# Tile 41's first head, kept apart whole and made in ten pieces behind tiles 37 to 46

## The chip, the cores and the metric

The kernel runs on one core of a Trainium2 chip. A core has five engines with instruction streams of their own: TensorE (PE, matmuls, with PEld for its weight loads), VectorE (DVE), ScalarE (ACT), GpSimd (POOL) and SyncE (SP), which here only issues DMA transfers. PE writes to PSUM, a small memory that DMA can't read, so that results are copied from there to SBUF by ACT or DVE and sent to HBM from SBUF by 16 DMA engines. The engines wait for each other by semaphores alone. The metric is the device time of one execution in microseconds; for the kernel before it is 300.72 us (median of 3 runs, 300.61 to 300.89).

## The reference

```python
def setup_inputs():
    batch, n_heads, seq_t, seq_s, channels = 8, 12, 512, 512, 64
    ...

def reference(x: np.ndarray, y: np.ndarray) -> np.ndarray:
    return np.einsum('bhtc,bhsc->bhts', x, y).astype(np.float32)
```

For each of the 96 heads (batch by head), x is 512x64, y is 512x64, and the output is x times y transposed, 512x512 in float32. 25 MB come in and 100 MB go out.

## The kernel before

**Tiling.** The 96 heads are cut into NG = 6 groups of G = 16. A group of x or of y is one load of 2 MB into a slot, 128 partitions by 16 KB; eight partitions hold one head. `compress` casts a loaded slot to bf16 into `keep`; `mix` copies x from there into `xb`, and `transposes` turns `xb` and the kept y into `xT` and `yT` with 32x32 block transposes on DVE. There are two of each buffer, for the two halves of a group (unit i, NH = 12 units; unit i uses buffer i % 2).

**An output tile** holds two heads: a unit gives V = 4 tiles, so there are 48, numbered 0 to 47 (`o`). The 64 channels of a head use half of the 128 rows of PE, the two heads of a tile use both halves, and the matmuls of a tile put the two heads' rows on alternate partitions. Tile o is made for k = 0 to 7: k 0 to 3 into the PSUM buffer pm0 and k 4 to 7 into pm1, four banks each, which together is all of PSUM. `four` issues the four matmuls of one buffer. `result` has ACT copy pm0 and then pm1 into a slot of 2 MB, 128 partitions by 16 KB (L337), and `store` sends the slot to HBM from SP (L328). There are five slots for loads and results alike, so tile o waits for the store of tile o - 5.

**Order.** The instruction streams are written by hand: `emit` records for each step what it reads and writes, and puts in the waits that follow from that. ACT, DVE, POOL and SP get their instructions in program order. PE's are written last by `all_products`, a loop of six turns over eight tiles (j = o % 8), with register-valued waits on the semaphores `ev` (evictions by ACT) and `tr` (transposes). What doesn't fit the loop is recorded in `held` and issued inside an `If` on the turn.

**Tile 41** (SPLIT = 41) is stored in an own way. Its second head goes out of the slot as a whole (1 MB). Of its first head only k 0 and 1 go out of the slot (256 KB, pieces of 4 KB). The rest, k 2 to 7 (LEFT = 6), is made a second time by `corner`, right behind tile 41: three DVE copies pick single rows of x out of xT[0] into a piece of `keep` called `picked` (L275); 30 matmuls against the same y (L295) put these rows on chosen partitions, in eight groups of at most four that alternate between pm0 and pm1; DVE empties pm0 and ACT pm1 into `kept`, which lies over kept inputs that are no longer needed (L141 and L139); and three DMA issues (L314) send it: 4 partitions with 5 rows each from SP, 3 and 8 partitions with 4 rows each from POOL, in pieces of 12 KB (`FEW` has the partitions and the rows of each). The partitions are 0, 4, 8, 12; 20, 24, 28; and 64 to 92 in steps of 4; partition 16 is passed over. The eight groups are held behind tile 41's own products on PE, and a last wait in the held list keeps PE from tile 42's products until both buffers have been copied out. `prepare(i)` issues the transposes of unit i and the mixing copies of unit i + 1 on DVE; it stands behind the last tile of a unit, for the unit after the next.

Of the kernel before, what the change touches and what calls it, by code (L numbers as in the profile page):

```python
# [9 lines left out]
def kernel(  # L10
# [22 lines left out]
    nc = tc.nc  # L33
    B, H, T, C = x.shape
    _, _, S, _ = y.shape
# [3 lines left out]
    R = T // Q  # L39
    NG = B * H // G  # L40
# [5 lines left out]
    SLOTS = 5  # L46
    TURNS = NH // 2
    SPLIT = V * NH - 2 * V + 1
    LEFT = 6
    N = (K - LEFT) * S  # L50
    GROUP = 4
    FEW = ((0, 4, 5), (5, 8, 4), (16, 24, 4))
    fp32 = mybir.dt.float32
    bf16 = mybir.dt.bfloat16
    u32 = mybir.dt.uint32
# [52 lines left out]
    def emit(name, make, reads=(), writes=(), dma=None, lane=None, known_by=None, held=None):  # L108

        points = [writer[r] for r in (*reads, *writes) if r in writer]  # L110
        points += [v for w in writes for v in readers.get(w, ())]
        if name == "pool" and name in ticks:
            points.append((name, ticks[name]))
        need(name, points, known_by, held)
        p, step = (lane or name, 1) if dma is None else (f"dma{dma}", 16)
        if p not in sems:
            sems[p] = tc.alloc_semaphore(p)
        if held is not None:
            held.append(make)
        elif make is not None:  # L120
            make().then_inc(sems[p], step)
        at = (p, ticks.get(p, 0) + step)
        ticks[p] = at[1]
        snaps[at] = {**known[name], p: at[1]}
        if dma is None:
            for q in lanes.get(name, (name,)):
                snaps[at][q] = ticks.get(q, 0)
        for r in reads:
            readers.setdefault(r, []).append(at)
        for w in writes:  # L130
            writer[w], readers[w] = at, []

    made_slots, loaded, held = [], {}, []
    in_front = ["dve", "pool", "dve", "act"]

    def copy(name, dst, src, reads, writes):
# [9 lines left out]
    def both(i):  # L146
        return [("slot", i, 0), ("slot", i, 1)]
# [92 lines left out]
    def all_products():  # L240

        with nc.tensor.Fori(0, TURNS, 1) as t:
            for j in range(2 * V):
                if j % V == 0:
                    nc.tensor.wait_ge(sems["tr"], t * 2 + j // V + 1)
                for pm in range(2):
                    nc.tensor.wait_ge(sems["ev"], t * (4 * V) + 2 * j + pm + 1)
                    four(j, pm).then_inc(sems["pe"], 1)
                if j == SPLIT % (2 * V):
                    with nc.tensor.If(t == SPLIT // (2 * V)):  # L250
                        for step in held:
                            if callable(step):
                                step().then_inc(sems["pe"], 1)
                            else:
                                nc.tensor.wait_ge(sems[step[0]], step[1])

    def corner():

        half, h = divmod(SPLIT % (2 * V), V)
        xT = xTs[half].bitcast(bf16).rearrange("p (k h q u) -> p k h q u", k=K, h=V, u=2)  # L260
        yT = yTs[half].bitcast(bf16)
        most = max(many for _, _, many in FEW)
        kept = keep[:, :most * LEFT * S].bitcast(fp32)
        runs = kept.rearrange("p (j n) -> p j n", j=most)
        dst = ov[SPLIT // V, h][:, 0, N:]
        picked = keep[:, 3 * NG * R // 2 * D:].bitcast(bf16)[:, :most * LEFT * 96].rearrange(
            "p (j k m) -> p j k m", j=most, k=LEFT
        )
        under = [("yb", 1, b, ch) for b in range(NG - 3, NG - 1) for ch in range(2)]
        first = 0  # L270
        for lo, hi, many in FEW:
            rows = (hi - lo) * many
            emit(
                "dve",
                lambda: nc.vector.tensor_copy(  # L275
                    picked[:, :many, :, 4 * lo:4 * hi:4],
                    xT[:, K - LEFT:, h, first:first + rows, 0].rearrange("p k (e j) -> p j k e", j=many),
                ),
                [("xT", half)],
                [("picked", lo)] + (under if lo == 0 else []),  # L280
            )
            first += rows
        places = [[("xk", i)] for i in range(NG - 1)]
        for i in range(0, NG - 1, 2):
            places.append([("yb", 0, b, ch) for b in (i, i + 1) if b < NG - 1 for ch in range(2)])
        banks = [divmod(b, LEFT) for b in range(most * LEFT)]
        for g in range(0, len(banks), GROUP):
            part = banks[g:g + GROUP]
            pm = g // GROUP % 2
            m = 96 if part[0][0] < most - 1 else 16  # L290

            def make(part=part, pm=pm, m=m):

                for b, (j, k) in enumerate(part):
                    last = nc.tensor.matmul(  # L295
                        pms[pm][:m, b, :], picked[:, j, k, :m], yT[:, h * S:(h + 1) * S],
                        start=True, stop=True,
                    )
                return last

            emit("pe", make, [("picked", lo) for lo, _, _ in FEW] + [("yT", half)], [("pm", pm)], held=held)
            copy(
                "act" if pm else "dve", kept[:m, g * S:(g + len(part)) * S],
                pms[pm].rearrange("p j s -> p (j s)")[:m, :len(part) * S],
                [("pm", pm)], places[g // GROUP],
            )
        need("pe", [v for pm in range(2) for v in readers[("pm", pm)]], held=held)
        first = 0
        for lo, hi, many in FEW:
            rows = (hi - lo) * many  # L310
            name = "pool" if lo else "sp"
            emit(
                name,
                lambda: engines[name].dma_start(  # L314
                    dst[first:first + rows].rearrange("(e j) n -> e j n", j=many),
                    runs[4 * lo:4 * hi - 3:4, :many],
                ),
                reads=[w for place in places for w in place],
                dma="side" if lo else "corner",
            )  # L320
            first += rows

    def store(o, s):
        i, h = divmod(o, V)
        to, src = ov[i, h], slots[s]
        parts = [(to, src)] if o != SPLIT else [(to[:, 1], src[1::2]), (to[:, 0, :N], src[0::2, :N])]
        for to, src in parts:
            emit("sp", lambda: nc.sync.dma_start(to, src), reads=both(s), dma=s)  # L328

    def result(o, s):  # L330

# [22 lines left out]
    with tc.tile_critical():  # L354
        sems["ev"] = tc.alloc_semaphore("ev")
        ticks["ev"] = 2
        nc.scalar.sem_inc(sems["ev"], 2)
        for g in range(SLOTS):
            load(g)
        emit(  # L360
            "pool",
            lambda: nc.gpsimd.dma_start(  # L362
                spare[0:17:4, :, :D // 2], xv[0, 0:5].rearrange("p (a b c) -> p a b c", a=2, c=D)[:, :, 0, :D // 2]
            ),
            writes=["spare"],
            dma="side",
        )
        for half, name in enumerate(("dve", "pool")):
            emit(
                name,  # L370
                lambda: engines[name].memset(xbs[half], 0.0),  # L371
                writes=[("xb", half, part) for part in range(4)],
            )
        front = []
        for n in range(2 * NG):
            if n == 11:
                result(3, slot())
            compress(n)
            mix(n // 4, "pool", n % 4)
            if n == 4:  # L380
                transposes(0)
            if n < 5:
                load(n + SLOTS)
            elif n in (6, 8):
                load(n // 2 + 7)
            elif n < 10:
                front.append(slot())
            if n > 7 and n < 11:
                result(n - 8, front[n - 8])
            if n == 9:  # L390
                transposes(1)
        prepare(2)
        for o in range(V, V * NH):
            result(o, slot())
            if o == SPLIT:
                corner()
            if o % V == V - 1:
                prepare(o // V + 2)
        all_products()
        need("pool", [("dmaside", ticks["dmaside"])])  # L400
        need("dve", [("dmacorner", ticks["dmacorner"])])
        for i, name in enumerate(("dve", "dve", "dve", "dve", "act")):
            need(name, [(f"dma{i}", ticks[f"dma{i}"])])
# [30 lines left out]
```

## Time and profile before

| | us |
|---|---|
| median of 3 runs | 300.72 (300.61 to 300.89) |
| the profiled execution | 300.63 |
| its span | 298.8 |
| ACT busy | 217.9 (73%) |
| DVE busy | 161.6 (54%) |
| PE busy | 144.7 (48%) |
| POOL busy | 57.9 (19%) |
| DMA, mean rate over the span | 421 GB/s |
| granted TensorE clock, mean | 0.773 |

The span goes from the first to the last instruction of the program; the device time has some more around it. Lines of the profile name an engine, an operation, output<-input by the program's names, and shapes. "L141" is the line of a helper (`copy`), which all copies share, so these are told apart by their tiles and shapes: `keep<-pm` is a copy of the corner, `xb<-keep` one of `mix`, `keep<-slot` one of `compress`. "L139" is the same helper's branch for ACT. In the timeline, a line gives start, length, engine, line, operation and count, and in brackets how long the engine had been idle and what ended that.

### The profile page before, as it was taken

Reading aid. Unit: us, or ns where it says so; the run is one execution under the profiler, and the core shown is the slowest. Engines: PE = TensorE matmul, PEld = TensorE weight load, DVE = VectorE, ACT = ScalarE, POOL = GpSimd, SP = SyncE. Lnnn points to the kernel's source line nnn. Section 1 sums busy time; section 2 is a strip of 40 time slices with the busy share of each in tenths; the row PEclk is TensorE's granted clock in tenths of the full one; section 3 lists DMA queues with packets and bytes.
Section 4 is the critical chain, followed back from the end, with each engine's and each line's share of the span. In section 5 each row is a group of like instructions: output and inputs, shape, how many; then the busy total and the mean of one; then the engine's idle time right before and its main releaser. Section 6 shows DMA issues by size and latency. Waiting matters only on the chain.

```text
span 298.8 us, 1363 instructions
## 1 busy us (share of the span) xinstructions
PE 144.7 (48%) x408; PEld 39.3 (13%) x414; DVE 161.6 (54%) x80; ACT 217.9 (73%) x113; POOL 57.9 (19%) x26
## 2 busy tenths in 40 slices
PE   0000040547665663867475665676475667475400
PEld 0000010111111110211111111111111112121100
DVE  2167897999929594915809439076292535600000
ACT  1665676999999996786868686767777775589900
POOL 3399999991000000000000000000000000010000
PEclk9999995657789997565956767756857767979965
DMA  7999999999999999999999999999999999999997
GB/s 265 430 428 432 430 430 428 428 432 432 425 432 430 434 428 429 434 430 428 430 432 429 432 436 428 430 436 423 425 432 434 430 421 428 421 388 430 421 421 316
DMA packets 8875, 125.87 MB, mean 421 GB/s; under 512 B 1128, under 2 KB 1128, under 8 KB 1192
## 3 DMA queue, kind: packets, MB, share of 16 engines
q1 hardware_dynamic: 8680, 125.29, 98.6%
q0 software_dynamic: 192, 0.54, 0.5%
q8 instruction: 1, 0.02, 0.0%
q14 instruction: 2, 0.02, 0.0%
HBM read 25.17 MB, written 100.66 MB: 421 GB/s over the span
## 4 chain that ended last, share of the span: by engine, by line
DMA 54%; ACT 27%; issue 5%; PE 4%; DVE 3%; another core or an unknown queue 1%; SPq 0%; ACTq 0%
DMA out_dram<-slot 41%; ACT slot L337 25%; DMA slot<-in_y_dram 7%; DMA slot<-in_x_dram 6%; DVE keep L141 3%; ACT keep L139 2%; PE pm L295 2%; PE pm L234 2%; SPq L157 0%; ACTq L101 0%; SPq L429 0%; SPq L354 0%
## 5 line engine op out<-in xcount | busy, mean ns | idle before, releaser
L337 ACT ACTIVATE slot<-pm 128x2048 f32<-128x2048 f32 x96 | 173.7, 1894 | 38.2 <-DMA out_dram<-slot 35.0
L234 PE MATMUL pm<-yT,xT 128*128 128x512 bf16 x378 | 135.6, 502 | 132.0 <-ACT slot L337 92.4
L206 DVE STREAM_TRANSPOSE xT<-xb 128x2048 uint32<-128x2048 uint32 x12 | 46.8, 3897 | 69.4 <-PE pm L234 67.0
L234 PEld LDWEIGHTS pm<-yT,xT 128*128 128x128 bf16 x384 | 35.9, 114 | 230.7 <-ACT slot L337 152.0
L139 ACT ACTIVATE keep<-slot 128x4096 bf16<-128x4096 f32 (+1 forms) x12 | 36.5, 3044 | 21.5 <-DMA slot<-in_x_dram 16.3
L141 DVE COPY xb<-keep 32x2048 bf16<-32x2048 bf16 x36 | 47.0, 1305 | 1.0
L141 DVE CAST keep<-slot 64x2048 bf16<-64x2048 f32 x12 | 36.1, 3010 | 17.1 <-DMA slot<-in_y_dram 16.9
L314 POOL DMA_DIRECT2D out_dram<-keep x2 | 1.1, 558 | 192.6 <-DVE keep L141 192.6
L141 POOL COPY xb<-keep 32x2048 bf16<-32x2048 bf16 x12 | 36.2, 3017 | 9.2 <-ACT keep L139 8.4
L215 DVE STREAM_TRANSPOSE yT<-keep 128x1024 uint32<-128x1024 uint32 x12 | 23.1, 1928 | 0.0
L141 POOL CAST keep<-slot 64x2048 bf16<-64x2048 f32 x6 | 17.8, 2973 | 1.4 <-DMA slot<-in_y_dram 0.8
L141 DVE COPY keep<-pm 96x2048 f32<-96x2048 f32 (+1 forms) x4 | 9.1, 2285 | 10.5 <-PE pm L295 10.5
L295 PE MATMUL pm<-yT,keep 128*96 128x512 bf16 (+1 forms) x30 | 9.2, 446 | 4.9 <-DVE keep L141 2.8
L139 ACT ACTIVATE keep<-pm 96x2048 f32<-96x2048 f32 (+1 forms) x4 | 6.6, 1657 | 5.4 <-PE pm L295 5.4
L295 PEld LDWEIGHTS pm<-yT,keep 128*96 128x96 bf16 (+1 forms) x30 | 3.4, 130 | 11.0 <-DVE keep L141 4.5
L371 DVE MEMSET xb<- 128x2048 uint32 x1 | 1.8, 1765 | 1.4 <-SPq L354 1.4
L139 ACT ACT_TABLE_LOAD x1 | 1.3, 1283 | 1.0 <-SPq L354 1.0
L371 POOL MEMSET xb<- 128x2048 uint32 x1 | 1.8, 1823 | 0.0
L362 POOL DMA_DIRECT2D spare<-in_x_dram x1 | 0.7, 701 | 1.2 <-SPq L354 1.2
L275 DVE COPY keep<-xT 128x120 bf16<-128x120 bf16 (+2 forms) x3 | 0.7, 355 | 0.0
L418 POOL MEMSET const-float32-0.0<- 128x1 f32 x1 | 0.1, 98 | 0.2 <-issue 0.2
L418 POOL MEMSET const-float32-1.0<- 128x1 f32 x1 | 0.1, 98 | 0.0
(2 smaller groups left out, 0.2 us busy)
## 6 DMA issues: line engine op xcount, KB each, us to landing
out_dram<-slot SPq DMA_DIRECT2D x47, 2048.0 KB, 20.5
slot<-in_x_dram SPq DMA_DIRECT2D x6, 2048.0 KB, 17.7
slot<-in_y_dram SPq DMA_DIRECT2D x6, 2048.0 KB, 20.8
out_dram<-slot SPq DMA_DIRECT2D x1, 1024.0 KB, 16.9
out_dram<-keep POOLq DMA_DIRECT2D x1, 384.0 KB, 6.1
out_dram<-slot SPq DMA_DIRECT2D x1, 256.0 KB, 18.6
out_dram<-keep SPq DMA_DIRECT2D x1, 240.0 KB
out_dram<-keep POOLq DMA_DIRECT2D x1, 144.0 KB, 5.6
```

The costliest lines, as they stand in the source:

```text
L139: lambda: nc.scalar.activation(dst, src, COPY)
L141: else engines[name].tensor_copy(dst, src),
L206: lambda: nc.vector.transpose(xTs[half].rearrange("p (k r e) -> p k e r", k=K, e=E), xbs[half].rearrange("p (k e c) -> p k e c", k=K, e=E),),
L215: lambda: nc.vector.transpose(yTs[half].rearrange("p (r j) -> p j r", r=D), ybs[half][b].rearrange("p (j c) -> p j c", c=D),),
L234: last = nc.tensor.matmul(pms[pm][:, b, :], xT[:, 4 * pm + b, h, :], yT[:, h * S:(h + 1) * S], start=True, stop=True,)
L275: lambda: nc.vector.tensor_copy(picked[:, :many, :, 4 * lo:4 * hi:4], xT[:, K - LEFT:, h, first:first + rows, 0].rearrange("p k (e j) -> p ...
L295: last = nc.tensor.matmul(pms[pm][:m, b, :], picked[:, j, k, :m], yT[:, h * S:(h + 1) * S], start=True, stop=True,)
L314: lambda: engines[name].dma_start(dst[first:first + rows].rearrange("(e j) n -> e j n", j=many), runs[4 * lo:4 * hi - 3:4, :many],),
L337: lambda: nc.scalar.activation(slots[s][:, k * S:(k + 4) * S], pms[pm].rearrange("p j s -> p (j s)"), COPY),
L362: lambda: nc.gpsimd.dma_start(spare[0:17:4, :, :D // 2], xv[0, 0:5].rearrange("p (a b c) -> p a b c", a=2, c=D)[:, :, 0, :D // 2]),
L371: lambda: engines[name].memset(xbs[half], 0.0),
L418: nc = _bacc.Bacc("TRN2", target_bir_lowering=False, num_devices=1)
```

## The change

`LEFT` is gone: all eight k of tile 41's first head are kept apart (1 MB, pieces of 16 KB), and `store` sends only the second head of tile 41 out of the slot. `corner` is split in three. `pick` copies the rows of x for all eight k, behind tile 35 and its `prepare`; `picked` now lies in `xb[0]`, whose last use is over by then. `piece(o)` stands behind each of the tiles 37 to 46 (BEGIN = 37, GROUPS = 10): four matmuls into pm0, one copy of pm0 by DVE into `kept`, and a wait of PE for that copy. The last two pieces have 16 rows, the others 96. `send` issues the three kept stores behind tile 46. `held` has one list for each of the ten tiles, each in an `If` of its own in PE's loop.

```diff
-    LEFT = 6
-    N = (K - LEFT) * S
     GROUP = 4
+    BEGIN = SPLIT - 4
     FEW = ((0, 4, 5), (5, 8, 4), (16, 24, 4))
+    GROUPS = -(-max(many for _, _, many in FEW) * K // GROUP)
...
-                if j == SPLIT % (2 * V):
-                    with nc.tensor.If(t == SPLIT // (2 * V)):
-                        for step in held:
-                            if callable(step):
-                                step().then_inc(sems["pe"], 1)
-                            else:
-                                nc.tensor.wait_ge(sems[step[0]], step[1])
+                for o in held:
+                    if o % (2 * V) == j:
+                        with nc.tensor.If(t == o // (2 * V)):
+                            for step in held[o]:
+                                if callable(step):
+                                    step().then_inc(sems["pe"], 1)
+                                else:
+                                    nc.tensor.wait_ge(sems[step[0]], step[1])
...
+    kept = keep[:, :most * K * S].bitcast(fp32)
+    picked = xbs[0].bitcast(bf16)[:, :most * K * 96].rearrange(
+        "p (j k m) -> p j k m", j=most, k=K
+    )
...
+    def piece(o):
...
+        g = o - BEGIN
+        part = [divmod(b, K) for b in range(most * K)][g * GROUP:(g + 1) * GROUP]
+        m = 96 if part[0][0] < most - 1 else 16
...
+            for b, (j, k) in enumerate(part):
+                last = nc.tensor.matmul(
+                    pms[0][:m, b, :], picked[:, j, k, :m], yT[:, h * S:(h + 1) * S],
+                    start=True, stop=True,
+                )
...
+        emit(
+            "pe", make, [("picked", lo) for lo, _, _ in FEW] + [("yT", half)], [("pm", 0)], held=held[o]
+        )
+        copy(
+            "dve", kept[:m, g * GROUP * S:(g * GROUP + len(part)) * S],
+            pms[0].rearrange("p j s -> p (j s)")[:m, :len(part) * S],
+            [("pm", 0)], places[g],
+        )
+        need("pe", readers[("pm", 0)], held=held[o])
...
-        parts = [(to, src)] if o != SPLIT else [(to[:, 1], src[1::2]), (to[:, 0, :N], src[0::2, :N])]
-        for to, src in parts:
-            emit("sp", lambda: nc.sync.dma_start(to, src), reads=both(s), dma=s)
+        if o == SPLIT:
+            to, src = to[:, 1], src[1::2]
+        emit("sp", lambda: nc.sync.dma_start(to, src), reads=both(s), dma=s)
...
             result(o, slot())
-            if o == SPLIT:
-                corner()
+            if BEGIN <= o < BEGIN + GROUPS:
+                piece(o)
+            if o == BEGIN + GROUPS - 1:
+                send()
             if o % V == V - 1:
                 prepare(o // V + 2)
+            if o == BEGIN - 2:
+                pick()
```

## The prediction

> **What bounds the kernel now.** I read the page's forty slices first, then the windows, then the timeline of ScalarE (ACT) and of the last third, and last the chain that ended last. The slices say that the DMA engines are the bound:
>
> ```profile
> PEclk9999995657789997565956767756857767979965
> DMA  7999999999999999999999999999999999999997
> GB/s 265 430 428 432 430 430 428 428 432 432 425 432 430 434 428 429 434 430 428 430 432 429 432 436 428 430 436 423 425 432 434 430 421 428 421 388 430 421 421 316
> ```
>
> All 16 DMA engines are busy from the second slice to the last, at about 430 GB/s. Only one slice, at 261 to 269 us, falls to 388. The windows put the hole there (columns: window, its length, busy us and count of PE, PEld, DVE, ACT, POOL, then granted clock, DMA share, GB/s):
>
> ```profile
> 125.00:224.00 99.00, 62.10 (x162) 15.80 (x164) 55.12 (x32) 73.82 (x41) 0.00 (x0) 0.69 1.01 430
> 265.00:270.00 5.00, 3.19 (x13) 0.93 (x12) 0.00 (x0) 5.00 (x4) 0.00 (x0) 0.95 0.84 347
> ```
>
> A full DMA share reads 1.01, so 5.00 x (1.01 - 0.84) / 1.01 = 0.8 us of DMA time were lost there, and nowhere else after the start. The timeline of ACT, which makes every output tile, shows why:
>
> ```profile
> 224.80 3.65 ACT L337 ACTIVATE slot<-pm 128x2048 f32<-128x2048 f32 x2 [1.31 <-DMA out_dram<-slot]
> 229.70 3.65 ACT L337 ACTIVATE slot<-pm 128x2048 f32<-128x2048 f32 x2 [1.25 <-DMA out_dram<-slot]
> ...
> 244.49 3.65 ACT L337 ACTIVATE slot<-pm 128x2048 f32<-128x2048 f32 x2 [1.30 <-DMA out_dram<-slot]
> 249.99 1.87 ACT L139 ACTIVATE keep<-pm 96x2048 f32<-96x2048 f32 x1 [1.85 <-PE pm L295]
> ...
> 262.71 21.35 ACT L337 ACTIVATE slot<-pm 128x2048 f32<-128x2048 f32 x12 [2.51 <-remote]
> ```
>
> Tiles 37, 38 and 41 start at 224.80, 229.70 and 244.49. A tile takes ACT 3.65 us, then ACT sits idle until a slot is free: each tile waits for the store of five tiles earlier, and these land 4.9 us apart. Behind tile 41 come the eight groups of the corner, and tile 42 starts only at 262.71, 18.2 us after tile 41 where 4.9 was the pace. That nearly costs nothing because the stores run far ahead:
>
> ```profile
> 223.52 20.89 DMA out_dram<-slot
> 244.41 0.02 issue
> ```
>
> This is the chain of waits: tile 36's store was issued at 223.52 and landed at 244.41, four stores deep in the queue. Its sixteen landings in the trace run from 242.23 to 244.41. A store onto an empty queue takes less: tile 42's, issued at 266.38, has its first packets 1.87 us later and lands at 273.17, 6.8 in all. So after tile 37's store (issued 228.47) the fastest DMA engine had 242.23 - 1.87 - 228.47 = 11.9 us in hand before tile 38's store was needed. This **lead** is what the corner spends, and what the change spends.
>
> **The change, part by part.** The question is how long a tile takes when a piece stands behind it, and whether ten such tiles spend more than the lead. The parts have these rows:
>
> ```profile
> 218.65 1.89 PE L234 MATMUL pm<-yT,xT 128*128 128x512 bf16 x4 [0.64 <-ACT slot L337]
> 246.51 1.03 PE L295 MATMUL pm<-yT,keep 128*96 128x512 bf16 x4 [1.38 <-ACT slot L337]
> 247.59 2.29 DVE L141 COPY keep<-pm 96x2048 f32<-96x2048 f32 x1 [6.16 <-PE pm L295]
> ...
> 258.76 2.28 DVE L141 COPY keep<-pm 16x2048 f32<-16x2048 f32 x1 [1.12 <-PE pm L295]
> 261.40 0.84 PE L234 MATMUL pm<-yT,xT 128*128 128x512 bf16 x3 [2.25 <-DVE keep L141]
> ```
>
> Four matmuls take 1.03 us at the full clock and 1.89 at half, 1.08 and 1.93 to the start of what waits for them. A copy out of PSUM on DVE takes 2.29 us whether 96 or 16 partitions are used.
>
> Every piece goes through pm0, the PSUM half that also takes k 0 to 3 of every tile, and the held list ends with a wait of PE for that copy. So from one tile's first eviction to the next tile's first eviction stand in one chain, each waiting for the one before: ACT empties pm0 (1.88); PE enters the branch (0.14, from ACT's end at 246.37 to 246.51); four matmuls of the piece; DVE copies (2.29); PE leaves the branch and starts the next tile (0.36, from 261.04 to 261.40); four matmuls of the tile; ACT may start. Behind PE's wait are all of the next tile's products, those into pm1 too. ACT's second eviction lies beside the piece and costs nothing. Fixed part: 1.88 + 0.14 + 2.29 + 0.36 = 4.67. The two groups of four depend on the clock: 6.83 us a tile at the full clock, 8.53 at half. In 125 to 224 us, with eight matmuls in 4.9 us, the granted clock was 0.69; the chain has twelve in about 7.8, nearly the same density with gaps of the same kind. I take that row: 0.69 is half clock for 62% of the time, 0.62 x 1.93 + 0.38 x 1.08 = 1.61 a group, and the **cycle** is 4.67 + 3.21 = 7.88 us, against the 4.9 at which the DMA engines take a tile away.
>
> Other edits. The three picks move from behind tile 40's preparation to tile 35's and take 8 planes in place of 6: 0.73 x 8 / 6 = 0.97 us on DVE, behind the mixing copies that end at 225.84. They end at 226.8 where the first piece could start at 224.80 + 1.88 + 0.14 = 226.82: nothing, at worst 0.3. The transposes for tiles 44 to 47 (3.88 + 1.90 us) stand on DVE between the copies of pieces 39 and 40; the second copy would be ready 0.36 + 1.61 + 1.88 + 0.14 + 1.61 = 5.6 us after the first, so it waits 0.2 (1.3 at full clock, 0 at half). The four copies taken from ACT (6.6 us) were inside the corner and go with it. Tile 41's 256 KB part goes from SP's queue and its bytes come with the kept rows: the bytes in all are the same. The three kept stores move from behind tile 41 to behind tile 46. On SP the kept store waits for piece 46's copy, 1.88 + 0.14 + 1.61 + 2.29 = 5.9 us after tile 46's first eviction starts; only tile 47's store is behind it, which isn't ready before 7.88 + 3.67. On POOL only its final wait is behind the two others.
>
> What they do to the end: tile 46's store is issued 3.67 us after its first eviction starts (228.47 against 224.80) and, onto an empty queue, lands 6.8 later. SP's kept store is 4 partitions of five 16 KB pieces. A tile is 8 packets of 16 KB on each of 16 engines in 4.9 us, 0.61 each; how the 4 partitions are spread no row shows. Spread over all engines the 320 KB take 0.8 us, on one engine each 3.06. The 5 landings of the 240 KB store of before (four of them data) are nearest to one engine each, so I take 3.06. Then tile 47's store takes 4.9. From tile 46's start to the last landing: 3.67 + 6.8 + 3.06 + 4.9 = 18.4.
>
> The **sum**: tile 37 starts at 224.80 as before, since up to there only untaken branches are new, on a PE that waits for ACT. Nine cycles, 70.9, and 0.2 for the transposes: tile 46 starts at 295.9. The last landing is at 314.3 where it was 297.68, so 16.6 later. Span 298.8 + 16.6 = 315.4; the profiled execution took 300.63 for a span of 298.8, so 1.83 more: **317.3 us**. That execution stands 0.09 under the median of the runs, 300.72. Cross-check by the lead: nine tiles lose 7.88 - 4.9 each, 26.8; the lead pays 11.9, less 2.45 for tile 41's store, which is half as long; a hole of 17.4 us opens. All at full clock: 61.5 + 1.3, end 306.0, 309.0 us. All at half: 76.8, and tile 47's own cycle decides (8.53 + 3.67 + 6.8 = 19.0): end 320.6, 323.5 us.
>
> **The rivals.** *Full clock.* The same chain at 6.83 us, 309.0 us. For it: in the corner and after it the clock was 0.84 to 1.00, with gaps of 1.3 to 2.3 us between groups. Against it: there PE was denser (33 matmuls in the 16 us from 246, against 12 in 7.9 here), and at the pace of 125 to 224, where the gaps in the timeline are 0.6 to 2.1 us, it was 0.69. The Trainium skill (TensorE: Matmul & The Clock Gate, "HAM oscillation — how this bites in real kernels") has it that PE stays warm while no idle gap exceeds about 3.4 us; by that rule, with the longest gap here at 2.7 us, the full clock would hold and the time would be 309. The trace of before speaks against the rule as a sufficient one.
>
> *Half clock throughout*: 323.5. For it, the wider gaps; against it, the clock records go up to full every 10 to 14 us even at the pace of before.
>
> *The pieces hide* (not slower). ACT is idle 1.3 us a tile, DVE for 9 us at a time, and 11.9 us of lead stand ready. If the cycle stayed under (297.7 - 18.4 - 224.80) / 9 = 6.06 us, the DMA engines would never run dry, the hole of 0.8 us would close and the time be 299.8 to 300.6. It needs 0.8 us less than the full-clock cycle, so a step must leave the chain: PE not waiting for the copy, say. Against it: the wait is in the held list, and no row of the chain can overlap another on the same half of PSUM.
>
> **How the numbers follow.** Mixed clock 0.75, full clock 0.13, half clock 0.08, hidden 0.04, shared between faster and no change. A measurement of this kernel tells about 0.2% (0.6 us) from no change. Every clock gives slower, so slower is 0.96. The range goes from just under the full-clock end to just under the half-clock end, 308 to 322.
>
> **What would show it.** Right: ACT's first evictions of tiles 38 to 47 about 7.9 us apart with PE as what ended their idle time, not the DMA; a granted clock near 0.7 there; DMA share under 0.8 from about 265 us on; tile 47's store issued near 307; the kept stores behind tile 46's. Wrong: evictions still 4.9 us apart (the pieces hide), or a cycle under 7 with the clock at 0.9 (full clock), or a last landing more than 4 us after tile 47's store should have landed (the kept stores cost more than one engine's five packets).

## The result, and the profile after

The changed kernel takes 324.89 us (median of 6 runs, 324.12 to 326.14) against 300.67 for the kernel before (6 runs, 300.55 to 300.97): a ratio of 1.0805, 95% interval 1.0784 to 1.0826. It is slower, as forecast, but by 24 us and not by 17, and beyond the upper end of the range. The profiled execution took 324.97 us, its span is 323.1.

The forty slices of the changed kernel:

```profile
PEclk9999999996999996568567765765677777777655
DMA  7999999999999999999999999999999965666771
GB/s 284 432 426 430 434 428 424 430 430 434 426 430 434 426 435 426 434 430 432 431 426 436 424 436 430 428 434 428 424 424 430 428 290 241 278 260 260 322 265 63
```

Up to slice 32, 258 us, the DMA engines are as full as before. Then they run at 241 to 322 GB/s for seven slices, and in the last one nearly dry. The timeline of ACT from tile 36 on gives the reason for the first part (start, length, and in brackets how long ACT had been idle and what ended it):

```profile
219.86 3.65 ACT L347 ACTIVATE slot<-pm 128x2048 f32<-128x2048 f32 x2 [1.25 <-DMA out_dram<-slot]
224.80 3.65 ACT L347 ACTIVATE slot<-pm 128x2048 f32<-128x2048 f32 x2 [1.29 <-DMA out_dram<-slot]
233.68 3.65 ACT L347 ACTIVATE slot<-pm 128x2048 f32<-128x2048 f32 x2 [5.23 <-PE pm L234]
241.65 3.65 ACT L347 ACTIVATE slot<-pm 128x2048 f32<-128x2048 f32 x2 [4.32 <-PE pm L234]
...
296.50 3.65 ACT L347 ACTIVATE slot<-pm 128x2048 f32<-128x2048 f32 x2 [3.92 <-PE pm L234]
304.06 3.65 ACT L347 ACTIVATE slot<-pm 128x2048 f32<-128x2048 f32 x2 [3.92 <-PE pm L234]
```

From tile 38 on ACT no longer waits for a store but for PE. Tile 46 starts at 296.50: nine cycles of 7.97 us in the mean, against 4.9 before. The chain that ended last shows one such cycle link by link (start, length, what; L347 is ACT's emptying, L234 a tile's matmuls, L297 a piece's):

```profile
288.94 1.89 ACT slot L347
290.87 1.04 PE pm L297 x4
291.93 2.29 DVE keep L141
294.22 0.35 issue
294.57 1.90 PE pm L234 x4
296.50 1.89 ACT slot L347
```

ACT empties pm0, PE makes the piece, DVE copies it out, PE leaves the branch, PE makes the next tile's half, ACT may start: no link of this chain lies beside another. The end of the kernel is in the windows (after the length come busy us of the five engines, then granted clock, DMA share, GB/s):

```profile
306.00:310.00 4.00, 0.00 (x0) 0.00 (x0) 0.00 (x0) 1.71 (x1) 0.00 (x0) 0.50 0.67 266
310.00:314.00 4.00, 0.00 (x0) 0.00 (x0) 0.00 (x0) 0.00 (x0) 0.00 (x0) 0.50 1.08 381
314.00:318.00 4.00, 0.00 (x0) 0.00 (x0) 0.00 (x0) 0.00 (x0) 0.00 (x0) 0.50 0.21 78
318.00:321.50 3.50, 0.00 (x0) 0.00 (x0) 0.00 (x0) 0.00 (x0) 0.00 (x0) 0.50 0.16 70
```

From 318 us a DMA share of 0.16 is left: some three of the 16 engines still work. Tile 47's store was issued at 307.73, and its sixteen landings in the trace are eight at 314.2 to 314.4, four at 315.5 to 316.7, one at 318.1 and three at 321.9. One of the last three engines carried this, from the trace's packets, joined where one starts as another ends:

```
queue   bytes        start    end
POOL's  65536        306.37   309.27
SP's    40960        309.27   310.79
SP's    40960        310.79   312.31
POOL's  65536        312.30   316.68
SP's    16384 x 8    316.69   321.55
```

Two of the eleven runs of 64 KB that POOL's two kept stores consist of, this engine's share of SP's kept store between them, and then the eight packets of tile 47. In the kernel before the kept pieces were 12 KB each; here the rows of a partition touch each other in `kept` and in the output, and the build made one run of 64 KB (POOL) or two of 40 KB (SP) out of them.

### The profile page after: what moved, and what is told of

The parts are those of the page before. It is cut to its first block, busy times and chain, and to the rows that moved or that the text cites. A ratio compares the mean times of both kernels' runs of the same rounds, so it can differ in the third digit from the quotient of the medians.

```text
span 323.1 us, 1437 instructions
## 1 busy us (share of the span) xinstructions
PE 156.3 (48%) x412; PEld 43.7 (14%) x424; DVE 175.5 (54%) x86; ACT 211.9 (66%) x109; POOL 57.9 (18%) x26
## 4 chain that ended last, share of the span: by engine, by line
DMA 43%; ACT 22%; DVE 12%; PE 12%; issue 5%; SPq 0%; ACTq 0%; DVEq 0%
DMA out_dram<-slot 30%; ACT slot L347 20%; DVE keep L141 9%; PE pm L234 8%; DMA slot<-in_y_dram 6%; DMA slot<-in_x_dram 6%; PE pm L297 4%; ACT keep L139 2%; DVE xb L141 2%; DVE xT L206 1%; DVE yT L215 1%; SPq L157 0%; DVE xb L277 0%; ACTq L101 0%; SPq L443 0%
## 5 line engine op out<-in xcount | busy, mean ns | idle before, releaser
L347 ACT ACTIVATE slot<-pm 128x2048 f32<-128x2048 f32 x96 | 174.3, 1885 | 73.6 <-PE pm L234 43.4
L234 PE MATMUL pm<-yT,xT 128*128 128x512 bf16 x372 | 143.8, 537 | 143.4 <-ACT slot L347 77.8
L234 PEld LDWEIGHTS pm<-yT,xT 128*128 128x128 bf16 x384 | 39.1, 121 | 244.8 <-ACT slot L347 126.9
L141 DVE COPY keep<-pm 96x2048 f32<-96x2048 f32 (+1 forms) x10 | 22.9, 2285 | 45.7 <-PE pm L297 45.7
L297 PE MATMUL pm<-yT,xb 128*96 128x512 bf16 (+1 forms) x40 | 12.5, 442 | 5.6 <-ACT slot L347 3.3
L297 PEld LDWEIGHTS pm<-yT,xb 128*96 128x96 bf16 (+1 forms) x40 | 4.6, 138 | 16.4 <-ACT slot L347 10.5
L277 DVE COPY xb<-xT 128x160 bf16<-128x160 bf16 (+2 forms) x3 | 1.0, 425 | 0.0
```

Of the source, the lines that this page charges most:

```text
L141: else engines[name].tensor_copy(dst, src),
L234: last = nc.tensor.matmul(pms[pm][:, b, :], xT[:, 4 * pm + b, h, :], yT[:, h * S:(h + 1) * S], start=True, stop=True,)
L277: lambda: nc.vector.tensor_copy(picked[:, :many, :, 4 * lo:4 * hi:4], xT[:, :, h, first:first + rows, 0].rearrange("p k (e j) -> p j k e", ...
L297: last = nc.tensor.matmul(pms[0][:m, b, :], picked[:, j, k, :m], yT[:, h * S:(h + 1) * S], start=True, stop=True,)
L347: lambda: nc.scalar.activation(slots[s][:, k * S:(k + 4) * S], pms[pm].rearrange("p j s -> p (j s)"), COPY),
```

## The experiments

The first eight tell apart what the cycle and what the end cost; the last looks for a version that is faster than both. The kernel before took 300.42 to 300.55 us in the median on the same chips, 300.07 to 302.00 in single runs. Where no number of runs is given, a version ran once, so a few tenths say nothing there.

**1. A gap between the kept rows.** 32 words after each row, so that rows no longer merge.

```diff
-    kept = keep[:, :most * K * S].bitcast(fp32)
+    PITCH = K * S + 32
+    kept = keep[:, :most * PITCH].bitcast(fp32)
...
-            "dve", kept[:m, g * GROUP * S:(g * GROUP + len(part)) * S],
+            "dve", kept[:m, g // 2 * PITCH + g % 2 * GROUP * S:g // 2 * PITCH + (g % 2 + 1) * GROUP * S],
...
-        runs = kept.rearrange("p (j n) -> p j n", j=most)
+        runs = kept.rearrange("p (j n) -> p j n", j=most)[:, :, :K * S]
```

> The changed kernel with 32 words left free between the kept rows, so that the kept stores go out as pieces of 16 KB and not as runs of 64 and 40 KB that were merged over rows. Theory: tiles 37 to 46 are made at the pace of before (71.7 us from tile 37's first eviction to tile 46's), and the 7.3 us by which the last store landed later than foreseen are two runs of 64 KB (2.90 and 4.38 us) on each of three DMA engines that also carry 80 KB of SP's kept store. In pieces they spread, and the time falls from 325.0 to 317.7 (317.0 to 318.5), with the last store's sixteen landings within 1 us. Rival: the tail is long because the kept stores stand last, ahead of tile 47's store, whatever their form: 324 to 326.

Measured: 317.78 us, the last store's landings from 314.2 to 314.8, tile 46 again at 296.49. So 7.2 us of the loss belong to the form of the kept stores, and 17.2 are left for the cycle. The windows of this run have no thin tail:

```profile
310.00:314.00 4.00, 0.00 (x0) 0.00 (x0) 0.00 (x0) 0.00 (x0) 0.00 (x0) 0.50 0.97 410
314.00:315.90 1.90, 0.00 (x0) 0.00 (x0) 0.00 (x0) 0.00 (x0) 0.00 (x0) 0.50 0.00 0
```

**2. No pieces.** On top of the first: `pick` and `piece` return at once.

> As the first, but the picks, the ten groups of matmuls and their copies are left out; the kept stores send what lies in their place. Theory: nothing is left in the chain between two tiles, the tiles come at 4.9 us, the DMA engines never run dry, and the time is 299.8 to 300.8. Rival: the kept stores behind tile 46 or the branches cost something by themselves: 303 or more.

Measured: 300.41 us. The tiles come 4.9 us apart again, with the stores as what ends ACT's waits:

```profile
259.89 3.65 ACT L353 ACTIVATE slot<-pm 128x2048 f32<-128x2048 f32 x2 [1.27 <-DMA out_dram<-slot]
264.79 3.65 ACT L353 ACTIVATE slot<-pm 128x2048 f32<-128x2048 f32 x2 [1.25 <-DMA out_dram<-slot]
```

So the loss of the cycle comes with the pieces. Of the kept stores this run says less. Only SP's stands behind tile 46 here: POOL has no copies left to wait for, and its two were issued at 75 us. The fourth run is nearer: POOL's are issued at 277 us, some 5 us ahead of tile 46's store, and SP's behind it, all in pieces of 16 KB. POOL's issues in this run and in the fourth:

```profile
75.14 1.11 POOL L330 DMA_DIRECT2D out_dram<-keep  x2 [6.43 <-ACT keep L139]
```

```profile
277.20 1.11 POOL L328 DMA_DIRECT2D out_dram<-keep  x2 [208.57 <-DVE keep L141]
```

The fourth run takes 300.14 us, so kept stores in pieces of 16 KB, issued that late, cost nothing that can be told. The second run is also a bound: without any hole in the DMA engines' work, and with ten groups less, its time can't be told from before.

**3. Half of each copy**, on the changed kernel itself.

```diff
-            "dve", kept[:m, g * GROUP * S:(g * GROUP + len(part)) * S],
-            pms[0].rearrange("p j s -> p (j s)")[:m, :len(part) * S],
+            "dve", kept[:m, g * GROUP * S:g * GROUP * S + len(part) * S // 2],
+            pms[0].rearrange("p j s -> p (j s)")[:m, :len(part) * S // 2],
```

> The changed kernel, but each copy of a piece on DVE takes only the first half of its columns (the other half is not copied). Theory: the copy is a link of the chain from tile to tile, so 2.29 us become about 1.2, nine times: 9.8 us less, 315.2 (314 to 316.5), and the cycle falls from 7.9 to 6.8 us. Rival: the pace is set by PE (its clock and its branches) and the copy lies beside it: 323 or more.

Measured: 312.66 us, 12.3 less and not 9.8. The copy took 1.22 us, 1.07 less, as the theory has it; but the mean cycle fell by 1.36, from 7.97 to 6.61. The other 0.29 is PE's: with less time between its groups the granted clock rose, and the tile's four matmuls took 1.53 us in the mean where they took 1.83, while the piece's stayed at 1.32. The windows of the changed kernel (from 224) and of this run (from 225):

```profile
224.00:245.00 21.00, 11.47 (x31) 3.64 (x30) 8.46 (x8) 10.64 (x6) 0.00 (x0) 0.72 1.01 429
245.00:270.00 25.00, 14.17 (x36) 4.55 (x36) 13.68 (x6) 11.23 (x7) 0.00 (x0) 0.73 0.76 323
```

```profile
225.00:265.00 40.00, 22.62 (x69) 7.53 (x68) 15.60 (x13) 21.87 (x12) 0.00 (x0) 0.80 1.01 427
```

So the copy is a link of the chain, and the shorter link paid a second time here, by the clock. The rival falls.

**4. Five pieces**, behind every second tile.

```diff
-            if BEGIN <= o < BEGIN + GROUPS:
+            if BEGIN <= o < BEGIN + GROUPS and (o - BEGIN) % 2 == 0:
```

> As the first, but with only the pieces behind tiles 37, 39, 41, 43 and 45 (the other five are left out). Theory: a tile with a piece takes 7.9 us, one without 3.5 to 4.0 as it is behind; tile 46 starts at 279 to 281 us, just where the lead of the stores is used up, and the time is 300.4 to 302.0: half the pieces cost almost nothing. Rival: every piece costs its delay, in proportion: half of the loss, 309.

Measured: 300.14 us, a little under the expected range; proportion would have been 309. ACT's timeline:

```profile
224.91 3.65 ACT L351 ACTIVATE slot<-pm 128x2048 f32<-128x2048 f32 x2 [1.29 <-DMA out_dram<-slot]
234.76 7.18 ACT L351 ACTIVATE slot<-pm 128x2048 f32<-128x2048 f32 x4 [6.20 <-PE pm L234]
...
278.66 7.19 ACT L351 ACTIVATE slot<-pm 128x2048 f32<-128x2048 f32 x4 [3.40 <-PE pm L234]
```

A tile with a piece takes 6.8 to 9.9 us, the next one 3.5, and the mean from tile 37 to 46 is (278.66 - 224.91) / 9 = 5.97, just under the 6.06 that the prediction gave as the point from which a cycle costs. The lead of the stores pays for these delays whole. With ten pieces it was used up by about 259 us, where the DMA share of the changed kernel first falls under 1, and the delays behind that were paid in full.

**5. The outer dimension of POOL's stores.** On top of the first: four stores of 3 partitions and four of 8, one piece of 16 KB from each partition, in place of 12 and 32 rows.

```diff
+            for js in [slice(0, many)] if not lo else [slice(j, j + 1) for j in range(many)]:
...
-                    dst[first:first + rows].rearrange("(e j) n -> e j n", j=many),
-                    runs[4 * lo:4 * hi - 3:4, :many],
+                    dst[first:first + rows].rearrange("(e j) n -> e j n", j=many)[:, js],
+                    runs[4 * lo:4 * hi - 3:4, js],
```

> As the first experiment (16 KB pieces, a gap between the kept rows), but POOL's two kept stores are issued as four of 3 partitions and four of 8 partitions, one piece of 16 KB from each partition, so that the store has the partitions as its outer dimension, as the changed kernel's has, at the piece size of the first experiment. Theory: the outer dimension decides which DMA engines a store uses; 3 and 8 partitions go to the same first engines as SP's four, three engines get eight pieces more, the last store's landings spread over about 5 us again, and the time is 317.8 + 8 x 0.61 = 322.7 (322 to 324.5). Rival: the size of the runs (64 KB) made the tail, not where they went: 317.5 to 319.

Measured: 324.59 us. With every packet at 16 KB the tail is back, three engines at 320.7 to 320.8 and one at 320.3 while the other twelve landed by 317.2. So the tail doesn't need the large runs: it comes from where the packets go, and that follows the outer dimension. 3 and 8 partitions share engines, 12 and 32 rows spread. That they share them with SP's four is the reading of the packets above. The Trainium skill (DMA: Bandwidth & Descriptors, "Why a DMA increments its semaphore by 16 and not by 1") says that a DMA uses the largest k up to 16 engines that divides the outer dimension on both sides, on SP's queue the lowest-numbered; the four data landings of SP's kept store agree. No run here gives the engines' numbers, and how POOL's queue chooses its engines is known here from the packets and landings alone. The time is 1.9 us over the expected 322.7, which stays unexplained; the run also issues eight stores from POOL where the first issues two.

**6. All ten groups behind tile 41**, in pm0 and pm1 by turns, DVE and ACT emptying them, on top of the first.

```diff
-            if BEGIN <= o < BEGIN + GROUPS:
-                piece(o)
-            if o == BEGIN + GROUPS - 1:
-                send()
+            if o in BURSTS:
+                for n, g in enumerate(BURSTS[o]):
+                    piece(o, g, n % 2)
+                need("pe", [v for pm in range(2) for v in readers[("pm", pm)]], held=held[o])
+            if o == max(BURSTS):
+                send()
```

Here `BURSTS = {41: range(10)}`, and `piece` takes the group, the PSUM buffer and with it the engine.

> As the first experiment, but all ten groups stand behind tile 41, in pm0 and pm1 by turns, DVE emptying the one and ACT the other, as the kernel before does with its eight, and the kept stores follow. Theory: a group costs 1.8 us there instead of 3.0 to 3.4, because copies and matmuls of two groups overlap; no tile is made for 18.3 us instead of 14.6, the hole of before grows by the 3.7, and the time is 304.2 (303.5 to 305). Rival: the cost is in the groups and not in how they are chained, ten of them cost about what they cost one by one: 314 or more.

Measured: 304.43 us; tile 41 ends at 248.23 and tile 42 starts at 266.56, 18.3 us for ten groups.

```profile
266.56 21.66 ACT L350 ACTIVATE slot<-pm 128x2048 f32<-128x2048 f32 x12 [1.54 <-PE pm L235]
```

The same work as in the first experiment, chained otherwise and with half of the copies on ACT, is 13.4 us faster.

**7. Two bursts**, `BURSTS = {37: range(0, 5), 43: range(5, 10)}`.

> As the sixth, but five groups behind tile 37 and five behind tile 43, the kept stores behind tile 43. Theory: five groups in a row keep the next tile back by 9 us, which the lead of 11.9 us covers, and six tiles in between at 3.5 us give it back before the second time; the DMA engines never run dry and the time is 300.0 to 300.5, a little under before. Rival: the lead is not given back in between or is shorter than read, a hole opens: 301.5 or more.

Measured: 302.55 us (6 runs), ratio 1.0074, interval 1.0056 to 1.0091. A miss. The first burst took from 228.25 to 241.96, 13.7 us, with a granted clock of 0.63 from 225 to 245, the second from 263.30 to 274.20, 10.9; 9 were foreseen for each. That is 2.7 and 2.2 us a group where ten groups in a row took 1.8. After the second the lead is gone:

```profile
275.00:280.00 5.00, 3.79 (x13) 0.96 (x11) 0.00 (x0) 5.00 (x4) 0.00 (x0) 0.78 0.54 226
```

**8. Two bursts with merged kept stores**, the same without the gap.

> As the seventh without the gap between the kept rows: the kept stores go out as runs of 64 and 40 KB again, but early, while the DMA queue is full. Theory: three engines still get 128 KB more than the others, and nothing evens that out before the end: 304.5 to 307.5. Rival: the merged runs cost only at the end of the kernel, where the other engines have nothing to do: 300.0 to 301.

Measured: 307.46 us, 4.9 over the seventh. The surplus of three engines stays with them to the end even when it is queued 30 us earlier, at a DMA share of 0.18 in the last 4.5 us. The rival falls.

```profile
300.00:304.50 4.50, 0.00 (x0) 0.00 (x0) 0.00 (x0) 0.00 (x0) 0.00 (x0) 0.50 0.18 76
```

**9. The kernel before with its corner in two bursts**, four groups behind tile 37 and four behind 43, the picks behind 35 and the kept stores behind 43; `corner` is cut at those places and `held` has two lists.

> The kernel before (k 2 to 7 kept apart, eight groups, 12 KB pieces), but four groups stand behind tile 37 and four behind tile 43, the picks behind tile 35 and the kept stores behind tile 43. Theory: the seventh run failed by the length of its bursts (13.7 and 10.9 us for five groups, where 9 were foreseen, against a lead of 11.9 less what tile 41's short store takes); four groups take some 10.5 and 8.7 us, tile 44 starts near 269.5 us, the DMA engines don't run dry, and the time is 299.9 to 300.6, at or a little under the kernel before. Rival: the first burst's delay is not made good over six tiles at 3.5 us each, and a hole opens: 301.3 or more.

Measured: 300.93 us (11 runs), ratio 1.0014, interval 1.0002 to 1.0025. The bursts took 9.0 and 7.3 us, no hole opened (DMA share 1.00 to 1.03 in every window of 5 us from 265 to 295), and the last landing came at 297.18 where it was 297.68 in the kernel before. The span is 298.3, but the execution took 300.94, above the expected 299.9 to 300.6: 2.6 us lie outside the span (2.4 to 2.9 in the eleven runs), where the kernel before has 1.8 and the changed one 1.9. What these 0.8 us are stays open, and no version here that makes the whole output is faster than the kernel before.

## Why the prediction was right, and where it failed

**The cycle was right.** Foreseen 7.88 us and tile 46 at 295.9; measured 7.97 and 296.50. Experiments 2, 3, 4 and 6 show that it is the chain over pm0: taken out, shortened, thinned out or overlapped, it gives the time back. Its links were less exact than the sum. Four matmuls were put at 1.61 us for the piece and for the tile alike; the piece took 1.32 in the mean of nine and the tile 1.83, because the granted clock was 0.86 in the mean during the piece's four, which follow the tile's eight closely, and 0.54 during the tile's four behind DVE's copy. Leaving the branch took 0.36 to 0.87, 0.50 in the mean, for the 0.36 of the one row there was, and entering it 0.05 for 0.14. That these misses and the first cycle's nearly cancel, so that the cycle is off by 0.09 only, is luck. So is a part of the clock: its row was chosen for a nearly equal density of matmuls, but 33 of them in 20 us, 67 in 40 and 66 in 40 went with a clock of 0.63, 0.71 and 0.77 (seventh run from 225 us, second and fourth from 225).

**The lead was right.** The fourth run puts the point where a cycle begins to cost at or over 5.97 us; 6.06 was worked out.

**The picks** were said to cost nothing, at worst 0.3. They started at 226.69 for 225.84, since the copies ahead of them ended later, and the first piece waited 1.0 us: that is the first cycle of 8.88. The transposes' 0.2 did not come: they ended at 252.52, and the copy of piece 40 started at 253.39.

**The step that failed** is the end: "From tile 46's start to the last landing: 3.67 + 6.8 + 3.06 + 4.9 = 18.4". It took 25.4 (321.92 - 296.50). Tile 46's store landed 10.48 after its start for 10.47 foreseen. SP's kept store took 1.53 + 1.51 = 3.04 us on one engine for 3.06. Tile 47's store took 4.9. What is missing are POOL's two kept stores, to which the sum gave no time at all: 2.90 + 4.38 = 7.3 us on three engines that also had SP's. The prediction said of them only what waits behind them on POOL's queue, not on which DMA engines their 704 KB would lie; for SP's store it asked that question. The sign of being wrong that it had named for this came true: tile 47's store landed 14.2 us after its issue, 7.4 more than the 6.8 of a store onto an empty queue. Experiment 1 takes these 7.3 us out and comes to 317.78, where the prediction had 317.3; experiment 5 brings the tail back by the outer dimension, with no packet over 16 KB.

**The range** failed with it. Both its ends were worked out from the clock, and the unknown place of the kept stores, which the text named for SP's, was not carried into it. The rule of the Trainium skill on idle gaps (TensorE: Matmul & The Clock Gate, "HAM oscillation — how this bites in real kernels"), which the prediction set against the trace, would have given the full clock. It did not hold here: the clock was 0.71 from 224 us to the last matmul at 305, with no gap of PE over 3.2 us.

## What to carry to other kernels

A pause in making tiles is free as long as the stores queued ahead cover it, and costs in full from there on, so compare the sum of all pauses with the lead, and not each with the pace. Work that passes through the buffer which the main loop also passes through adds its whole chain to the loop, while the same work through two buffers and two engines by turns took 1.8 us a group in one row of ten here, 2.7 and 2.2 in rows of five, where one by one each added 3.1 to a pace of 4.9. When a transfer changes its form, work out anew how many DMA engines take it and which: where two dimensions merge, the new outer one can pile a transfer onto engines that already have their share.

## What the runs showed of the hardware that was not expected

The time of a DMA run of 64 KB was not a fixed one: in the changed kernel it was 2.43 us on four engines and 2.90 on three at the same time, and 4.38 on three engines later, while on three other engines the packets of 16 KB went from 0.61 to 1.28 us. What links these is not shown.

The granted clock of PE changed in steps of 3.41 us, and what went with a change was how much of the step before it PE was busy. In all eleven traces, from 100 us on, it rose from half to full after steps in which PE's rows cover 0.78 or more of the time, and stayed at half after 0.80 or less; it fell to half after 0.46 or less, and stayed full after 0.45 or more. This is how 1.07 us less of DVE's time in a cycle could give 0.29 us of PE's besides, and why the number of matmuls alone need not tell the clock.
